# Index queries of rows 64 to 255 alone, and one more sum of four convolution tiles added by a transfer

## The chip, the cores and the metric

The kernel runs on one core of a Trainium2 chip. The metric is the device time of one execution in microseconds (us); a kernel is compared by the median of several executions. All times below are in microseconds unless marked ns.

## The reference

The layer works on 256 rows (tokens) of 1024 numbers in fp32. One projection of the normalized rows gives the inputs of two branches, their gates, and the *index* projections that choose keys:

```python
n = rmsnorm(x, g)
c_a, c_g, q, k, v, qi, ki, wi, gc, ga = split(n @ w_in)
u = c_a * sigmoid(c_g)                       # conv branch: 31 taps, one channel each
y_conv = silu(layernorm(conv31(u) + b)) @ w_conv_out
logits = einsum("bqhd,bsd->bqhs", qi, ki) * 64 ** -0.5     # 8 index heads of 64
score  = einsum("bqh,bqhs->bqs", wi * 8 ** -0.5, relu(logits))
score  = where(key <= query, score, -inf)
idx    = top_k(score, 64)                    # 64 keys for each query row
y_attn = attention(q, k, v over the chosen keys with idx <= query) @ w_attn_out
h = x + (sigmoid(gc + b1) * y_conv + sigmoid(ga + b2) * y_attn) @ w_mix_out
h = h + cross_attention(rmsnorm(h), rmsnorm(mem))          # 256 memory tokens, 4 heads
h = h + relu(rmsnorm(h) @ w1) ** 2 @ w2
out = rmsnorm(h)
```

The query of row r may see keys 0 to r. For rows 0 to 63 that is at most 64 keys, so the top 64 of them are all that they may see, whatever the scores are.

## The kernel before

**Products in two halves.** Every large product is of fp32 numbers written as a sum of two of TensorE's faster 32-bit format (fp32r): `hi`, a rounded copy, and `lo`, what is left. A weight chunk comes from HBM by a transfer on SyncE's queue into one of three buffers `raw`; ScalarE (ACT) copies each 128 columns of it to `hi` (`high`, L315), VectorE (DVE) subtracts to get `lo`. The normalized rows stand the same way in `n_p`, both parts side by side. A tile of 128 output columns takes eight passes over the 1024 inputs with `hi` weights against both parts of the rows (512 columns wide, 256 for each part) and eight *low* passes with `lo` weights against the high part alone (256 columns): `tile_b`, called by `form_b`. The two sums, in one PSUM bank, are put together by a copy on ACT (L481) and an addition on DVE (`merge`). `back` turns the order of passes: in every second tile the low passes come behind the first wide one and not at the end, so that a group of eight low passes of one tile is followed by one wide and the eight low passes of the next. Every instruction that the program gives to TensorE (PE) or DVE passes through a small counting class, so the profile puts all of them on L87; they are told apart by the names of their tiles.

**What runs beside what.** The weights are taken in a fixed order (`STREAM`): four conv tiles, the index queries `qi` (two chunks, four tiles `ps_qi`, L769 to L771), the index keys `ki`, four more conv tiles, the gates, v, then q and k head by head, memory keys and values, and so on to the feed-forward part. Behind each tile, `tick()` advances the side work that is under way by a step: the norm of the memory tokens (`memory`), index scores, attention heads, gates, merges. While a model of DVE's work is behind a model of PE's (`dve.total < pe.total - 1000`, where PE is priced at columns/2.4 ns), `tick` gives DVE the next conv *tap* (`acc<-u,cw,acc`, a multiply-add of a shifted tile) or a round of the choice of keys. Each engine then runs its own list in order, and waits by semaphores.

**The memory norm.** `memory` sums the squares of the memory rows on ACT, turns them to a mean on DVE (`ss_m`), takes the power −0.5 on GpSimd (POOL; `rs_m`, L629), and spreads the result over the partitions by two PE transposes into `ps_mrb`, whose copy (L631) goes on.

**The convolution's sums.** The 31 taps of the eight channel tiles are done in three ways. Most are taps on DVE. Some are products by ACT, two tiles at a time (`products`, L714), which a transfer of GpSimd's queue with an adding end puts onto `acc` (L715). And of tiles 4 to 7 the last 12 taps (`QUADS`) go through `four_tiles` (L673): ACT writes four products of one shift into a slot of `ring` (L683; two slots), and they are added to `four`. The first sums are added by DVE, the last `BY_DMA` = 3 (widths 228, 227 and 226) by transfers on GpSimd's queue (L689). At the end DVE adds `four` to `acc`, then the eight tiles are summed (`usum`) for the layer norm, which starts on PE with `ps_mub`.

**The choice of keys.** `index_scores` takes dot products of `qi_t` with the index keys `ki2`, for the first 128 queries (`qb` = 0) and the next, weights and sums them into `score`; `choose` finds the 64 largest in eight rounds on DVE, and `mask` turns what was found into a tile of large negative numbers `bias` (views of `picked`) that is added to the attention's scores; `causal` fills what lies ahead of the query.

Of the kernel before, what the change touches and what calls it, by code (L numbers as in the profile page):

```python
# [11 lines left out]
AF = mybir.ActivationFunctionType  # L12
ALU = mybir.AluOpType
# [3 lines left out]
P = 128  # L17
D = 1024
S = 256
KT = D // P  # L20
# [3 lines left out]
HD = 128  # L24
XH = 4
K_TOP = 64
IDX_SCALE = float((8 ** -0.5) * (64 ** -0.5))
ATT_SCALE = float(HD ** -0.5)
NEG_FILL = -1.0e38
NEG_TAKEN = -3.4e38  # L30
NEG_BIAS = -1.0e30
# [25 lines left out]
HALVES = 6  # L57
EARLY = (3,)
QUADS = 12
BY_DMA = 3  # L60
PACE = 5
WHOLE = (("conv", 0),)
SEVEN = tuple(range(1, 14))
# [28 lines left out]
class Parts:  # L92
# [5 lines left out]
    def of(self, part, kt, n):  # L98
        t = self.tiles[kt // 4][:, kt % 4 : kt % 4 + n, part, :]
        return t[:, 0, :] if n == 1 else t  # L100

    def high(self, kt, n=1):
        return self.of(0, kt, n)
# [18 lines left out]
def block_kernel(ctx, tc, x, xt, mem, memt, wst, wki, vecs, convw, gout, out):  # L122
    nc = tc.nc
    ctx.enter_context(tc.manual_schedule())
    pe = Counted(nc.tensor, pe_price)
    dve = Counted(nc.vector, dve_price)
    act = nc.scalar.activation
# [5 lines left out]
    lows = ctx.enter_context(tc.tile_pool(name="lows", bufs=HALVES))  # L133
# [4 lines left out]
    def t8(name, dt=F32, shape=(P, KT, S)):  # L138
        return big.tile(list(shape), dt, tag="t8", bufs=12, name=name)

    def parts_t8(name, nkt=KT):
        return Parts([t8(f"{name}{c}", F32R, (P, 4, 2, S)) for c in range(nkt // 4)])

    def w2(name, dt=F32, shape=(P, 512)):
        return work.tile(list(shape), dt, tag="w2", bufs=8, name=name)

    def w4(name, dt=F32, shape=(P, KT, P)):
        return work.tile(list(shape), dt, tag="w4", bufs=2, name=name)
# [4 lines left out]
    def ps_mm(name):  # L153
        return bank("mm", 2, name)
# [4 lines left out]
    def ps_aux(name):  # L159
        return bank("aux", 2, name)  # L160
# [3 lines left out]
    def ps_turn(name):  # L164

        mm_turn[0] += 1
        return (ps_mm if mm_turn[0] % 2 else ps_acc)(name)
# [156 lines left out]
    def split_high():  # L324
        if high_jobs and high_jobs[0].here() and (not high_jobs[0].slot or nsplit[0] - nused[0] < HALVES - held[0]):
            job = high_jobs.pop(0)
            nsplit[0] += job.slot
            while job.steps:
                job.step()
            job.high()  # L330

    def split_low():
        if low_jobs:
            low_jobs.pop(0)()
        for job in high_jobs[:3]:
            if job.steps and job.here():
                job.step()
                break
# [3 lines left out]
    def weights(kind, i, half, kt):  # L342

        key = (kind, i, half)
        while key not in prepared:
            split_high()
            split_low()
        nused[0] += key not in elsewhere
        return [w if kt is None else w.rearrange("p (k n) -> p k n", k=kt) for w in prepared.pop(key)]
# [9 lines left out]
    def add_some():  # L359
        if added and added[0][0] in ready and pe.total >= add_next[0]:  # L360
            pair, pause = added.pop(0)
            add_next[0] = pe.total + pause
            ready[pair]()
            if pair not in [p for p, _ in added]:
                held_back.append((pe.total + 10000, pair))
        if held_back and pe.total >= held_back[0][0]:
            fill.extend(queues.pop(held_back.pop(0)[1]))

    def split_ahead():
        split_low()  # L370
        split_high()

    def tick():
        for c in list(chains):
            if next(c, "end") == "end":
                chains.remove(c)
        while (len(fill) > 1 or (fill and (len(ended) > 5 or nused[0] < 5))) and dve.total < pe.total - 1000:
            fill_one()
        if fours and next(fours[0], "end") == "end":
            fours.clear()  # L380
        dve.total = max(dve.total, pe.total - 2000)
        add_some()

    def fill_one():

        some = [q for q in fill[:3] if q is not turn[0]] or fill
        q = some[0] if len(some[0]) < 10 and len(fill) > 3 else max(some, key=len)
        turn[0] = q
        q.pop(0)()
        if not q:  # L390
            fill.remove(q)
# [5 lines left out]
    def start(gen):  # L397
        chains.append(gen)
        return gen
# [13 lines left out]
    def tile_b(ps, w, x2, kts=range(KT), wide=False, late=False, back=False):  # L413

        ps = ps[: w[0].shape[2]]

        def lows(last):  # L420
            for kt in kts:
                pe.matmul(ps[:, S:], w[1][:, kt, :], x2.high(kt), start=False, stop=last and kt == KT - 1)

        if wide and not late:
            for kt in kts:
                pe.matmul(ps, w[0][:, kt, :], x2.both(kt), start=kt == 0, stop=back and kt == KT - 1)
                if back and kt == 0:
                    lows(False)
            if not back:
                lows(True)  # L430
            return
        for kt in kts:
            wh, wl = w[0][:, kt, :], w[1][:, kt, :]
            if not wide:
                mm_b(ps[:, :S], wh, wl, x2, kt, kt == 0, kt == KT - 1)
            elif kt == 0:
                pe.matmul(ps, wh, x2.both(kt), start=True, stop=False)
                pe.matmul(ps[:, S:], wl, x2.high(kt), start=False, stop=False)
            else:
                pe.matmul(ps[:, S:], wl, x2.high(kt), start=False, stop=False)  # L440
                pe.matmul(ps, wh, x2.both(kt), start=False, stop=kt == KT - 1)

    back = [False]

    def is_wide(kind, ct):

        return kind in ("f1", "qi", "gc", "ga", "ao", "xk", "q", "k") or (kind in ("mix", "co") and ct < 6)

    def form_b(kind, i, x2, after, ps_of=ps_mm):

        for ct in range(2):
            w = weights(kind, i, ct, KT)
            if (kind, i, ct) != ("mix", 3, 1):
                split_ahead()
            ps = ps_of(f"ps_{kind}{i}{ct}")
            wide = is_wide(kind, 2 * i + ct)
            tile_b(ps, w, x2, wide=wide, back=back[0])
            back[0] = wide and not back[0]
            after(2 * i + ct, ps if wide else ps[:, :S])
            tick()  # L460
# [28 lines left out]
    def copy_out(dst, ps, now=False):  # L489
        if ps.shape[1] == S:  # L490
            act(dst, ps, AF.Copy)
        elif now:
            merge_now(dst, ps)
        else:
            start(merge(dst, ps))

    def copy_to(dst):
        return lambda ct, ps: copy_out(dst[:, ct, :], ps)
# [27 lines left out]
    picked = w4("picked", F32, (P, D))  # L526
# [4 lines left out]
    ps = ps_aux("ps_warm")  # L531
# [30 lines left out]
    n2 = parts_t8("n_p")  # L562
# [8 lines left out]
    for rb in range(2):  # L571
        for kt in range(KT):
# [5 lines left out]
                             in1=x_rm[:, 1, D // 2 :], scale=1.0 / D, scalar=EPS, op0=ALU.mult, op1=ALU.add,  # L578
# [21 lines left out]
    for lo, hi in ((0, 1), (1, 2), (2, 4), (4, 6), (6, 8)):  # L600
        dve.tensor_tensor(out=n_f[:, lo:hi, :], in0=xg[:, lo:hi, :],
                          in1=rsb_n.unsqueeze(1).to_broadcast([P, hi - lo, S]), op=ALU.mult)
# [70 lines left out]
    def four_tiles(g):  # L673
# [6 lines left out]
        for n, s in enumerate(taps):  # L680
            dst = ring[:, n % 2, :, s:] if n else sums[:, :, s:]
            for t in range(4):
                act(dst[:, t, :], u[:, 4 * g + t, : S - s], AF.Copy, scale=cw[:, 4 * g + t, TAPS - 1 - s : TAPS - s])  # L683
                if (4 * n + t) % PACE != PACE - 1:
                    yield
            if 0 < n < QUADS - BY_DMA:
                dve.tensor_tensor(out=sums[:, :, s:], in0=sums[:, :, s:], in1=dst, op=ALU.add)
            elif n:
                nc.gpsimd.dma_start(sums[:, :, s:], dst, accum_op=ALU.add)  # L689
        s = taps[0]  # L690
        for _ in range(4 if BY_DMA else 1):
            yield
# [73 lines left out]
            start(memory())  # L766


    qi_t = t8("qi_t", F32, (P, 4, S))  # L769
    for i in range(2):  # L770
        form_b("qi", i, n2, copy_to(qi_t), ps_turn)  # L771
    wk = weights("ki", 0, 0, KT)
    split_ahead()
    ps = ps_mm("ps_ki")
# [3 lines left out]
    wi_t = w2("wi_t", F32, (P, S))  # L778
    act(wi_t[64:NK, :], ps[64:NK, :S], AF.Copy, scale=IDX_SCALE)
    tick()  # L780
    wi = cst.tile([P, 2, 8], F32, name="wi")

    bias = [picked[:, :P], picked[:, P : 3 * P]]
# [6 lines left out]
    def choose(qb, score):  # L790

        def turn(r):
            def go():
                m8 = small.tile([P, 8], F32, tag="m8", name=f"m8_{qb}_{r}")
                dve.max(out=m8, in_=score)
                dve.match_replace(out=score, in_to_replace=m8, in_values=score, imm_value=NEG_TAKEN)
                dve.total += 250
            return go

        def mask():  # L800
            dve.tensor_scalar(bias[qb], score, -3.3e38, NEG_BIAS, ALU.is_gt, ALU.mult)
            causal(bias[qb], qb, NEG_BIAS)

        return [turn(r) for r in range(K_TOP // 8)] + [mask]

# [417 lines left out]
    dst = open_banks("xo")  # L1223
    w = weights("xo", 0, 0, 1)
# [9 lines left out]
    w = weights("xo", 0, 1, 1)  # L1234
# [138 lines left out]
    class Hidden:  # L1373
# [7 lines left out]
        def after(self, ct, ps):  # L1381
            self.jobs.append(start(activation(self.c, ct % 2, ps, self.t, self.hi, self.lo)))
# [249 lines left out]
```

## Time and profile before

| What | us |
|---|---|
| median of 3 runs (497.07 to 497.12) | 497.12 |
| the profiled execution | 497.16 |
| its span, first to last instruction | 495.0 |
| TensorE busy | 487.3 |
| VectorE busy | 460.5 |
| ScalarE busy | 378.4 |
| GpSimd busy | 50.6 |

The mean granted clock of TensorE was 0.998. In rows of a timeline the columns are the start, the duration, the engine (PEld is TensorE's weight load), the line, the operation, what it writes and reads by the program's names, the shapes, and how many neighbours were put together; square brackets hold the engine's idle time just before and what ended it. A row of a tile or a line has the number of instructions and their least, middle and largest duration in ns. The chain gives the share of the span of each engine on the path that ended last.

### The profile page before, as it was taken

The page shows a single profiled execution, that of the slowest core. Times are in us where ns is not written, and L with a number is a line of the kernel's source. Part 1 is how long each engine was busy: PE and PEld are TensorE (multiplying, and loading weights), DVE is VectorE, ACT ScalarE, POOL GpSimd, SP SyncE. Part 2 cuts the span into 40 slices and gives each one's busy share as a digit, 9 for nine tenths or more (in the row PEclk, how much of TensorE's full clock was granted, in tenths as well). Part 3 has the DMA queues.
Part 4 walks back from the last instruction along what each step waited for, and adds up shares of the span by engine and source line. Part 5 has one row for each costly group of instructions (what it writes and reads, how often), then busy time and mean ns, then how long its engine had stood idle before and what let it go on. Part 6 is the DMA issues. An engine that isn't in the chain of part 4 may idle for free.

```text
span 495.0 us, 7793 instructions
## 1 busy us (share of the span) xinstructions
PE 487.3 (98%) x2832; PEld 429.2 (87%) x2832; DVE 460.5 (93%) x828; ACT 378.4 (76%) x678; POOL 50.6 (10%) x67
## 2 busy tenths in 40 slices
PE   8999999999999999999999999999999999999995
PEld 7888888888888889888889999988998888888884
DVE  4999999999999989989988987899999999999986
ACT  5778879999887786767846558687777878888852
POOL 2002212221111211000000000000010101121000
PEclk9999999999999999999999999999999999999999
DMA  8958676989887977354645552866979879999802
GB/s 318 354 215 276 180 190 198 304 245 253 277 219 223 246 176 213 115 171 175 250 169 183 209 204 87 290 189 138 253 274 292 237 242 262 294 333 314 256 9 85
DMA packets 33430, 110.36 MB, mean 223 GB/s; under 512 B 11104, under 2 KB 13408, under 8 KB 24432
## 3 DMA queue, kind: packets, MB, share of 16 engines
q1 hardware_dynamic: 24416, 93.03, 54.4%
q0 software_dynamic: 8688, 16.64, 17.2%
q8 instruction: 22, 0.36, 0.3%
q10 hardware_dynamic: 288, 0.20, 0.1%
q14 instruction: 16, 0.13, 0.1%
HBM read 99.29 MB, written 1.05 MB: 203 GB/s over the span
## 4 chain that ended last, share of the span: by engine, by line
PE 97%; DVE 1%; issue 0%; ACT 0%; DVEq 0%
PE ps_f L87 18%; PE ps_p L87 15%; PE ps_conv L87 9%; PE ps_co L87 5%; PE ps_mix L87 5%; PE ps_ao L87 5%; PE ps_k L87 5%; PE ps_ga L87 5%; PE ps_gc L87 5%; PE ps_q L87 5%; PE ps_v L87 4%; PE ps_xo L87 3%; PE ps_xq L87 2%; PE ps_xk L87 2%; PE ps_qi L87 2%; PE ps_xv L87 2%
## 5 line engine op out<-in xcount | busy, mean ns | idle before, releaser
L87 DVE TENSOR_TENSOR lo<-raw,hi 128x1024 fp32r<-128x1024 f32 x133 | 161.3, 1215 | 2.5 <-ACT hi L315 2.2
L315 ACT ACTIVATE hi<-raw 128x1024 fp32r<-128x1024 f32 x133 | 138.5, 1048 | 6.2 <-DMA raw<-in_wst_dram 6.1
L87 PE MATMUL ps_f<-ff_p,hi 128*128 128x512 f32 (+1 forms) x320 | 72.4, 347 | 0.0
L87 PEld LDWEIGHTS ps_f<-ff_p,hi 128*128 128x128 f32 x320 | 56.2, 189 | 8.2 <-ACT ft L1344 0.3
L87 DVE SCALAR_TENSOR_TENSOR acc<-u,cw,acc 128x241 f32<-128x241 f32 (+23 forms) x142 | 58.5, 465 | 0.1
L87 PE MATMUL ps_f<-ff_p,lo 128*128 128x256 f32 x256 | 46.8, 282 | 0.0
L87 PEld LDWEIGHTS ps_f<-ff_p,lo 128*128 128x128 f32 x256 | 39.3, 191 | 1.8
L715 POOL DMA_DIRECT2D acc<-products x25 | 21.7, 880 | 124.2 <-ACT products L714 59.5
L87 PE MATMUL ps_conv<-n_p,hi 128*128 128x512 f32 x112 | 29.2, 397 | 0.0
L87 PEld LDWEIGHTS ps_conv<-n_p,hi 128*128 128x128 f32 x112 | 20.4, 188 | 4.4 <-issue 0.3
L714 ACT ACTIVATE products<-u,cw 128x243 f32<-128x243 f32 (+19 forms) x50 | 22.1, 492 | 0.0
L293 ACT ACTIVATE inner<-sums 128x1024 fp32r<-128x1024 f32 x13 | 13.8, 1060 | 10.5 <-DVE sums L87 10.5
L87 DVE TENSOR_TENSOR ft<-ft 128x128 f32<-128x128 f32 (+2 forms) x49 | 19.4, 397 | 1.1 <-ACT ft L1344 0.6
L683 ACT ACTIVATE ring<-u,cw 128x236 f32<-128x236 f32 (+10 forms) x44 | 20.2, 480 | 0.0
L87 PE MATMUL ps_p<-outer,fs 128*128 128x512 f32 x78 | 20.1, 393 | 0.0
L87 PE MATMUL ps_v<-hi,n_p 128*128 128x512 f32 x64 | 19.9, 389 | 0.0
L87 PE MATMUL ps_p<-inner,fs 128*128 128x512 f32 x78 | 19.8, 389 | 0.0
L87 PE MATMUL ps_co<-u_p,hi 128*128 128x512 f32 (+1 forms) x80 | 19.3, 350 | 0.0
L87 PE MATMUL ps_mix<-mix_p,hi 128*128 128x512 f32 (+1 forms) x80 | 19.2, 349 | 0.0
L87 PE MATMUL ps_k<-n_p,hi 128*128 128x512 f32 x64 | 17.4, 403 | 0.0
L87 PE MATMUL ps_q<-n_p,hi 128*128 128x512 f32 x64 | 17.3, 402 | 0.0
L87 PEld LDWEIGHTS ps_p<-inner,fs 128*128 128x128 f32 x78 | 14.6, 188 | 3.0
(445 smaller groups left out, 1215.0 us busy)
## 6 DMA issues: line engine op xcount, KB each, us to landing
raw<-in_wst_dram SPq DMA_DIRECT2D x67, 1024.0 KB, 5.7
raw<-in_wst_dram SPq DMA_DIRECT2D x28, 512.0 KB, 6.7
sums<-in_wst_dram POOLq DMA_DIRECT2D x15, 512.0 KB, 8.0
acc<-products POOLq DMA_DIRECT2D x25, 256.0 KB, 5.5
x_rm<-in_x_dram SPq DMA_DIRECT2D x2, 512.0 KB, 4.0
mem_rm<-in_mem_dram SPq DMA_DIRECT2D x1, 1024.0 KB, 7.6
mem_t<-in_memt_dram SPq DMA_DIRECT2D x1, 1024.0 KB, 9.6
h_t<-in_xt_dram SPq DMA_DIRECT2D x1, 1024.0 KB, 7.0
```

The lines of the kernel that those rows point to most:

```text
L87: return fn(*args, **kwargs)
L293: act(hi, src, AF.Copy)
L315: act(hi, raw[:, ns], AF.Copy)
L683: act(dst[:, t, :], u[:, 4 * g + t, : S - s], AF.Copy, scale=cw[:, 4 * g + t, TAPS - 1 - s : TAPS - s])
L714: act(prod[:, a, s:], u[:, t, : S - s], AF.Copy, scale=cw[:, t, TAPS - 1 - s : TAPS - s])
L715: nc.gpsimd.dma_start(acc[:, ts, :], prod, accum_op=ALU.add)
```

## The change

The index queries of rows 0 to 63 are no longer computed (`FREE` = 64). A new `tile_behind` has the same order of passes as `tile_b` and the same turns of `back`, but takes the rows from 64 on: the wide passes read two pieces of 192 columns (384), the low ones 192. The merge has 192 columns. The first 64 rows of `qi_t` are set to zero once, and of the bias tile of the first 128 queries the rows 0 to 63 (`picked[:FREE, :P]`), by two memsets on GpSimd that wait for nothing; `mask` then writes rows 64 to 127 alone for `qb` = 0, and `causal` fills what lies ahead as before.

`BY_DMA` goes from 3 to 4: the sum of width 229 also leaves DVE and is added by a transfer from the ring's slot. The slots are the same two, so a slot that a transfer reads is written again when that transfer has landed.

Nothing else is written otherwise, but the model of `tick` counts the narrower passes as less PE work, so DVE's taps and ACT's `products` stand at other places in their lists behind the index queries.

```diff
+FREE = K_TOP
-BY_DMA = 3
+BY_DMA = 4
...
+    def behind(self, kt, row):
+        return self.tiles[kt // 4][:, kt % 4, :, row:]
...
+    def tile_behind(ps, w, x2, row, back=False):
+        both = ps.rearrange("p (a n) -> p a n", a=2)
+        def lows(last):
+            for kt in range(KT):
+                pe.matmul(both[:, 1, row:], w[1][:, kt, :], x2.high(kt)[:, row:], start=False, stop=last and kt == KT - 1)
+        for kt in range(KT):
+            lo = row
+            pe.matmul(both[:, :, lo:], w[0][:, kt, :], x2.behind(kt, lo), start=kt == 0, stop=back and kt == KT - 1)
+            if back and kt == 0:
+                lows(False)
+        if not back:
+            lows(True)
...
     qi_t = t8("qi_t", F32, (P, 4, S))
-    for i in range(2):
-        form_b("qi", i, n2, copy_to(qi_t), ps_turn)
+    nc.gpsimd.memset(qi_t[:, :, :FREE], 0.0)
+    nc.gpsimd.memset(picked[:FREE, :P], 0.0)
+
+    def query_part(dst, ps):
+        both = ps.rearrange("p (a n) -> p a n", a=2)[:, :, FREE:]
+        act(dst, both[:, 1, :], AF.Copy)
+        yield
+        dve.tensor_tensor(out=dst, in0=both[:, 0, :], in1=dst, op=ALU.add)
+
+    for ct in range(4):
+        w = weights("qi", ct // 2, ct % 2, KT)
+        split_ahead()
+        ps = ps_turn(f"ps_qi{ct}")
+        tile_behind(ps, w, n2, FREE, ct % 2 == 1)
+        start(query_part(qi_t[:, ct, FREE:], ps))
+        tick()
...
         def mask():
-            dve.tensor_scalar(bias[qb], score, -3.3e38, NEG_BIAS, ALU.is_gt, ALU.mult)
+            rows = slice(0 if qb else FREE, P)
+            dve.tensor_scalar(bias[qb][rows], score[rows], -3.3e38, NEG_BIAS, ALU.is_gt, ALU.mult)
             causal(bias[qb], qb, NEG_BIAS)
```

More of the change, by code (lines that the diff above doesn't have):

```diff
@@ L769, in block_kernel @@
     qi_t = t8("qi_t", F32, (P, 4, S))
-    for i in range(2):
-        form_b("qi", i, n2, copy_to(qi_t), ps_turn)
+    nc.gpsimd.memset(qi_t[:, :, :FREE], 0.0)
[12 more added lines that the diff above has]
+        tick()
+    assert not back[0]
     wk = weights("ki", 0, 0, KT)
```

## The prediction

> **What bounds the kernel now.** I read the page first (busy time, then the chain of waits), then the timeline of TensorE around the index queries, then the engines that feed it there, and last the stage in which the moved sum falls. All times are microseconds. The page says where the end comes from:
>
> ```profile
> PE 487.3 (98%) x2832; PEld 429.2 (87%) x2832; DVE 460.5 (93%) x828; ACT 378.4 (76%) x678; POOL 50.6 (10%) x67
> ...
> PE 97%; DVE 1%; issue 0%; ACT 0%; DVEq 0%
> ```
>
> TensorE (PE) is busy for 98% of the span and holds 97% of the chain that ended last. A microsecond taken from PE's stream comes off the end, unless PE then waits for something; a microsecond taken from VectorE (DVE) is worth nothing while PE is still fed. The profiled execution took 497.16, its span 495.0, so 2.16 lie outside the span; the median of the runs shown is 497.12, or 0.04 lower. The sum below is made against 497.16.
>
> The stage that the change narrows is that of the index queries, four tiles `ps_qi`. In PE's timeline the columns are start, duration, what ran, and how many:
>
> ```profile
> 31.80 1.98 PE L87 MATMUL ps_qi<-n_p,hi 128*128 128x512 f32 x8
> 33.61 1.12 PE L87 MATMUL ps_qi<-n_p,lo 128*128 128x256 f32 x8
> 34.56 0.40 PE L87 MATMUL ps_qi<-n_p,hi 128*128 128x512 f32 x1
> ...
> 39.18 1.11 PE L87 MATMUL ps_qi<-n_p,lo 128*128 128x256 f32 x8
> 40.24 0.43 PE L87 MATMUL ps_mrb<-ident,rs_m 128*128 128x128 f32 x2
> ```
>
> Passes overlap, so what a pass costs is its distance from the next start and not its duration: eight wide passes (33.61 − 31.80)/8 = 0.226 apart, eight low ones (34.56 − 33.61)/8 = 0.119 apart. The last eight low passes should therefore be through at 39.18 + 8 × 0.119 = 40.13, but `ps_mrb`, the next piece of work, starts at 40.24. That 0.11 is the only place in this stage where PE doesn't follow itself, and the forecast hangs on it. `ps_mrb` takes `rs_m` from GpSimd (POOL):
>
> ```profile
> 38.20 0.91 POOL L715 DMA_DIRECT2D acc<-products  x1 [30.33 <-ACT products L714]
> 38.84 1.35 POOL L629 TENSOR_TENSOR rs_m<-ss_m,half 128x2 f32<-128x2 f32 x1
> ...
> 228.94 0.71 POOL L538 TENSOR_TENSOR rs_vr<-ms_vr,half 128x2 f32<-128x2 f32 x1 [37.21 <-DVE ms_vr L87]
> ```
>
> `rs_m` ends at 38.84 + 1.35 = 40.19, and PE's next start is 0.05 later: PE already waits for GpSimd there. The same operation with nothing ahead of it (`rs_vr`) takes 0.71, so here it stood 0.6 behind the issue of the `acc` transfer.
>
> **The change, part by part. The wide passes.** 256 more columns cost 0.226 − 0.119 = 0.107, or 0.418 ns a column. 384 columns instead of 512 save 128 × 0.418 = 0.0535 a pass, × 8 = 0.43 a tile, 1.71 for four. That a pass now reads two pieces of 192 I price at nothing: a wide pass already reads two parts side by side.
>
> **The low passes.** 64 columns at the same rate would be 0.027 a pass. But each pass loads its own 128x128 weights, and other rows show what a pass costs that is narrower than its load: three passes of 128 columns and four loads beside passes of 2 columns (PEld is the weight load):
>
> ```profile
> 173.12 0.49 PE L87 MATMUL ps_pt<-ident,att_p 128*128 128x128 f32 x3
> ...
> L87 PE MATMUL ps_pt<-ident,att_p x24: 270/272/273, 168.7 to 215.4; 128*128 128x128 f32 x24
> ```
> ```profile
> 227.57 0.54 PEld L87 LDWEIGHTS ps_vr<-onesd,vs 128*128 128x128 f32 x4
> ...
> 40.24 0.19 PEld L87 LDWEIGHTS ps_mrb<-ident,rs_m 128*128 128x128 f32 x2
> ```
>
> One pass of 128 columns takes 0.27, three take 0.49, so they stand (0.49 − 0.27)/2 = 0.11 apart; with 2 columns the four loads stand at most (0.54 − 0.19)/3 = 0.117 apart. A narrower pass doesn't get under about 0.11. So a low pass saves 0.119 − 0.11 = 0.009, × 8 = 0.07 a tile and 0.29 for four; the ends are nothing and 0.86 (32 × 0.027), and I take 0.29, since 128 columns is the nearer row. The Trainium skill ("TensorE: Matmul & The Clock Gate", section "Back-to-back issue gap") gives an isolated gap of N/2.4 + 2.5 ns and says that in a stream weight load and pass set the spacing together. By the isolated gap alone (an estimate: 82.5 ns for 192 columns) a tile would gain 0.29 on these passes, and the forecast would come out 0.22 lower; the rows at 0.11 speak for the load.
>
> Together PE's own work shrinks by 1.71 + 0.29 = 2.0.
>
> **What of it is kept.** The order of PE's work around `ps_mrb` doesn't move. Before and now, from the last low passes of the third tile (`ps_qi` with a running number) to the fourth tile:
>
> ```order
> L87 MATMUL ps_qi_481<-n_p_125,lo_0_355 128x256 x4
> L87 MATMUL ps_mrb<-ident,rs_m 128x128 x2
> L87 MATMUL ps_qi_518<-n_p_124,hi_1_381 128x512
> L87 MATMUL ps_qi_518<-n_p_124,lo_1_382 128x256 x4
> L87 MATMUL ps_qi_518<-n_p_125,lo_1_382 128x256 x4
> ```
> ```order
> L88 MATMUL ps_qi_480<-n_p_125,lo_0_355 128x192 x4
> L88 MATMUL ps_mrb<-ident,rs_m 128x128 x2
> L88 MATMUL ps_qi_512<-n_p_124,hi_1_381 128x2x192
> L88 MATMUL ps_qi_512<-n_p_124,lo_1_382 128x192 x4
> L88 MATMUL ps_qi_512<-n_p_125,lo_1_382 128x192 x4
> ```
>
> Three tiles still stand ahead of `ps_mrb`, one behind it. PE will be there three tiles' gain, 3 × 0.50 = 1.50, sooner, so what decides is whether `rs_m` also comes sooner. It stands behind the `acc` issue on POOL's queue, which waits for `products` from ScalarE (ACT); its own input is `ss_m` from DVE:
>
> ```profile
> 36.48 0.36 ACT L481 ACTIVATE qi_t<-ps_qi 128x256 f32<-128x256 f32 x1
> 36.74 0.86 ACT L714 ACTIVATE products<-u,cw 128x236 f32<-128x236 f32 x2
> 37.51 1.05 ACT L315 ACTIVATE hi<-raw 128x1024 fp32r<-128x1024 f32 x1
> ```
> ```profile
> 36.15 1.63 DVE L87 SCALAR_TENSOR_TENSOR acc<-u,cw,acc 128x246 f32<-128x246 f32 x4
> ...
> 38.37 0.16 DVE L87 TENSOR_SCALAR ss_m<-ss_m 128x2 f32<-128x2 f32 x1
> ```
>
> ACT runs these one behind the other without a wait, so what releases `products` is ACT's own queue and not PE. The only thing that gets shorter in it is the copy of 192 instead of 256 columns: (1.05 − 0.36)/768 = 0.9 ns a column, × 64 = 0.06. `ss_m` was ready at 38.53, 0.31 before `rs_m` started. So `rs_m` ends at about 40.13 instead of 40.19, and of the 1.50 only 0.06 gets past `ps_mrb`. The fourth tile stands behind it and keeps its 0.50. **Sum: −0.06 − 0.50 = −0.56, 497.16 → 496.60.**
>
> DVE's order does move there. The planner counts PE's work cheaper and puts two conv taps behind `ss_m` that stood ahead of it; before and now:
>
> ```order
> L87 SCALAR_TENSOR_TENSOR acc<-u,cw,acc 128x250
> L87 SCALAR_TENSOR_TENSOR acc<-u,cw,acc 128x245
> L87 SCALAR_TENSOR_TENSOR acc<-u,cw,acc 128x249
> L87 TENSOR_TENSOR lo_0_415<-raw_236,hi_0_414 128x576
> L87 TENSOR_SCALAR ss_m<-ss_m 128x2
> ```
> ```order
> L88 SCALAR_TENSOR_TENSOR acc<-u,cw,acc 128x250
> L88 TENSOR_TENSOR lo_0_417<-raw_236,hi_0_416 128x576
> L88 TENSOR_SCALAR ss_m<-ss_m 128x2
> L88 TENSOR_TENSOR qi_t<-ps_qi_419,qi_t 128x192
> L88 SCALAR_TENSOR_TENSOR acc<-u,cw,acc 128x245
> ```
>
> `ss_m` comes two taps sooner, (1.63/4) × 2 = 0.8. That helps only if `ss_m` and not the `acc` issue holds `rs_m`; it is the first rival.
>
> **What is hidden.** The narrower merges (`qi_t`, 0.4 each on DVE) and the sum that leaves DVE free DVE time, which PE doesn't wait for:
>
> ```profile
> L87 DVE TENSOR_TENSOR four<-four,ring x8: 1104/1123/1129, 99.4 to 157.6; 128x944 f32<-128x944 f32 x1, 128x940 f32<-128x940 f32 x1, 128x936 f32<-128x936 f32 x1, 128x932 f32<-128x932 f32 x1
> ...
> DMA to landing us min/median/max: 5.4/6.2/10.5
> ```
>
> So 1.1 leaves DVE. The two memsets stand on POOL ahead of the first `products`, where it was idle for 30.33 before its `acc` issue. The planner's later taps fall due before the layer norm, whose `ps_mub` must not wait for `usum`:
>
> ```profile
> 216.29 0.87 DVE L87 TENSOR_TENSOR usum<-usum,acc 128x256 f32<-128x256 f32 x2
> ```
> ```profile
> 218.89 0.60 PE L87 MATMUL ps_mub<-usum,onesd 128*128 128x256 f32 x2
> ```
>
> `usum` ends 218.89 − 217.16 = 1.73 ahead. Three taps (0.41 each) and one more `usum` (0.43) now stand in DVE's order between the last attention output and `ps_mub`, where two `usum` stood: 1.66 instead of 0.87, and the 1.1 taken off DVE lies before them: covered. If that cover were gone, PE would lose tenths.
>
> **The rivals. R1, faster: `ps_mrb` waits less.** If `rs_m` is held by its input, it ends 0.8 sooner, and the sum is −0.56 − 0.8 = −1.36: 495.8. If it isn't held at all, the whole 2.0 comes through: 495.2. For it: the operation alone takes 0.71, not 1.35, and POOL's spans may hold waiting. Against: `ss_m` was 0.31 ahead, while `rs_vr` started 0.09 after its input,
>
> ```profile
> 228.70 0.15 DVE L87 TENSOR_SCALAR ms_vr<-ps_vr 128x2 f32<-128x2 f32 x1
> ```
>
> and the queue ahead of it has not moved. Chance 0.23.
>
> **R2, slower: the added transfer holds ACT.** POOL's queue late in the convolution, with what each issue waits for, before and now (a sum of four tiles is `four`, its columns at the end):
>
> ```order
> L715 DMA acc<-products 128x512 [waits DMASW6_49,Activation_49]
> L715 DMA acc<-products 128x512 [waits DMASW7_49,DMASW0_49,Activation_49]
> L715 DMA acc<-products 128x512 [waits DMASW0_49,Activation_49]
> L689 DMA four_923<-ring_924 128x4x228 [waits DVE_49,PE_49,Activation_49]
> L689 DMA four_923<-ring_924 128x4x227 [waits DMASW2_49,Activation_49]
> ```
> ```order
> L735 DMA acc<-products 128x512 [waits DMASW6_49,Activation_49]
> L709 DMA four_912<-ring_913 128x4x229 [waits DVE_49,DMASW0_49,PE_49,Activation_49]
> L735 DMA acc<-products 128x512 [waits DMASW7_49,Activation_49]
> L735 DMA acc<-products 128x512 [waits DMASW1_49,Activation_49]
> L709 DMA four_912<-ring_913 128x4x228 [waits DMASW0_49,Activation_49]
> L709 DMA four_912<-ring_913 128x4x227 [waits DMASW3_49,Activation_49]
> ```
>
> The 229 is new, between `acc` issues that stood together, and the 228 now has a landing (DMASW0) to wait for that it had not. With landings one behind another, what follows is late by one transfer. The profile of before has:
>
> ```profile
> 157.02 0.86 POOL L715 DMA_DIRECT2D acc<-products  x1 [5.62 <-ACT q L481]
> 161.66 0.86 POOL L715 DMA_DIRECT2D acc<-products  x1 [3.78 <-ACT products L714]
> 166.90 0.86 POOL L715 DMA_DIRECT2D acc<-products  x1 [4.38 <-DMA acc<-products]
> 167.44 1.66 POOL L689 DMA_DIRECT2D four<-ring  x1
> ```
> ```profile
> 180.45 0.86 ACT L683 ACTIVATE ring<-u,cw 128x226 f32<-128x226 f32 x2
> ...
> 183.69 0.49 ACT L955 ACTIVATE ptr<-ps_pt 128x384 f32<-128x384 f32 x1 [1.43 <-PE ps_pt L87]
> ```
> ```profile
> 186.95 0.83 PE L87 MATMUL ps_o<-ptr,v_rm 128*128 128x128 f32 x6
> ```
>
> The 228 issued at 167.44 landed at latest 10.5 on, at 177.9. One transfer more ahead of it, about 5 by the distance of the `acc` issues (4.64 and 5.24), makes 183, 182.4 with the 0.56; ACT's ring write of width 226 needs that slot at 180.45 − 0.56 = 179.9. So ACT will wait up to 2.5 in its queue, and behind it stand the next halves of weights and `ptr`, for which PE waits. The cover is ACT's idle 1.43 before `ptr` and the 186.95 − 184.18 = 2.77 from its end to `ps_o`, 4.2 in all. It decides from 4.2 of ACT's waiting, that is a landing past 184.1, and makes the kernel slower by more than 0.2% from 184.1 + 0.56 + 0.99 = 185.7. With the median 6.2 of `four` instead of 5 nothing shows; with its longest, 10.5, the landing is 187.9, PE waits 3.8, and the time is 496.60 + 3.8 = 500.4. Chance 0.09. The Trainium skill ("DMA: Bandwidth & Descriptors", section "Anatomy of one DMA — SWDGE (gpsimd) path") has 2.0 plus bytes/436e3, an estimate of 3.1 for these 0.47 MB; by that ACT would not wait at all, but the rows of this kernel start at 5.4.
>
> **R3, slower: narrow passes of this number format cost double.** No wide-format pass under 256 columns is in the trace. The plain fp32 product is:
>
> ```profile
> L87 PE MATMUL ps_conv<-xg,raw 128*128 128x256 f32 x32 | 7.3, 381 | 0.0
> ```
>
> 7.3/32 = 0.228 a record, two records a product, 1.78 ns a column. Should pieces of 192 fall to that rate, a low pass costs 0.34 instead of 0.119, 32 × 0.22 = 7.1 more, less 1.71: 502.5. Nothing in the trace asks for it. Chance 0.05.
>
> **How the numbers follow.** The forecast, 496.6 by 497.16 − 0.56 and 497.12 − 0.56, has 0.63. 0.2% (0.99, about what a measurement of this kernel can tell from no change) puts the bounds at 496.1 and 498.1, so the forecast counts as the same; R1 is faster, R2 and R3 slower. Chances: faster 0.23, same 0.63, slower 0.14. The range runs from R1's end with the whole gain, 495.2, to 497.6, where the early end of R2 costs a whole 1.0; the rest of the slower cases is left out.
>
> **What would show it right or wrong.** Right: in PE's timeline wide passes 0.172 and low ones 0.11 apart; PE idle for about 1.5 before `ps_mrb`, released by POOL's `rs_m` at about 40.13; the fourth tile 0.50 shorter; no idle PE near 184 to 187 and none before `ps_mub`. Wrong: `rs_m` ending before 39.5 (R1), ACT waiting more than 4.2 at a ring write with PE idle behind it (R2), low passes farther than 0.119 apart (R3), or PE idle at another place.

## The result, and the profile after

| | median | runs | lowest to highest |
|---|---|---|---|
| before | 497.12 | 12 | 496.94 to 497.73 |
| changed | 501.01 | 12 | 497.06 to 503.55 |

The measured ratio of changed to before is 1.006 (95% interval 1.0031 to 1.0089), and the medians lie 3.89 apart, 0.8%. The change is slower by either, and its median is outside the range that was given. It also spreads over 6.5 us, where the kernel before stays within 0.8. Ratios here and below leave out runs more than 1.5% above the fastest of their kernel and medians count all; on the chips of the experiments the kernel before, too, has a few runs at 501 to 504.4 with a clock of 0.992 to 0.995 (5 of 30, 4 of 36, 2 of 13), which widen the intervals there.

The 12 runs fall apart by their mean granted clock: two at 0.999 (497.06 and 497.43), six at 0.993 to 0.995 (498.84 to 501.97), four at 0.991 or 0.992 (502.25 to 503.55). The profiled one took 502.60, its span 500.5, clock 0.991. It shows two places where time and clock are lost. First the chain of its page and TensorE's waits (us in all, times, longest):

```profile
PE 86%; DVE 5%; DMA 3%; ACT 2%; issue 1%; POOL 1%; DVEq 0%; POOLq 0%; ACTq 0%
```
```profile
PE ps_o L88 <- ACT ptr L992: 2.1, 1, 2.1
PE ps_mrb L88 <- POOL rs_m L649: 2.1, 1, 2.1
```

Of the chain only 86% is TensorE's now, and there are two waits that before did not have. Here is TensorE at the index queries:

```profile
31.74 1.57 PE L88 MATMUL ps_qi<-n_p,hi 128*128 128x384 f32 x8
33.15 1.03 PE L88 MATMUL ps_qi<-n_p,lo 128*128 128x192 f32 x8
34.02 0.36 PE L88 MATMUL ps_qi<-n_p,hi 128*128 128x384 f32 x1
...
37.71 1.03 PE L88 MATMUL ps_qi<-n_p,lo 128*128 128x192 f32 x8
40.88 0.43 PE L88 MATMUL ps_mrb<-ident,rs_m 128*128 128x128 f32 x2 [2.13 <-POOL rs_m L649]
41.06 0.52 PE L88 MATMUL ps_qi<-n_p,hi 128*128 128x384 f32 x1
41.38 1.86 PE L88 MATMUL ps_qi<-n_p,lo 128*128 128x192 f32 x8
43.03 2.16 PE L88 MATMUL ps_qi<-n_p,hi 128*128 128x384 f32 x7
45.03 0.40 PE L88 MATMUL ps_ki<-n_p,hi 128*72 128x256 f32 x2
```

Wide passes stand (33.15 − 31.74)/8 = 0.176 apart, low ones (34.02 − 33.15)/8 = 0.109: a tile is 0.48 shorter. Then TensorE waits 2.13 for `rs_m`. But the eight low passes of the fourth tile take 1.86 where those of the third took 1.03, with no wait between them. The windows say why (columns: the window, its length, the busy times of PE, PEld, DVE, ACT and POOL with their numbers of instructions, then TensorE's granted clock as a share of the full one, the DMA share and GB/s):

```profile
31.70:38.58 6.88, 6.88 (x49) 6.83 (x48) 6.85 (x15) 6.85 (x15) 0.49 (x1) 1.00 0.60 194
38.58:40.88 2.30, 0.17 (x3) 0.01 (x1) 2.30 (x6) 1.01 (x2) 2.24 (x2) 1.00 1.00 367
40.88:42.00 1.12, 1.12 (x7) 1.12 (x7) 1.12 (x3) 0.66 (x2) 0.00 (x0) 0.67 0.79 219
42.00:43.00 1.00, 1.00 (x6) 1.00 (x6) 1.00 (x4) 1.00 (x3) 0.00 (x0) 0.50 0.83 260
43.00:44.00 1.00, 1.00 (x5) 1.00 (x4) 1.00 (x3) 0.69 (x2) 0.00 (x0) 0.50 0.88 299
44.00:45.00 1.00, 1.00 (x5) 1.00 (x5) 0.99 (x2) 0.00 (x0) 0.00 (x0) 0.67 1.04 285
45.00:46.00 1.00, 1.00 (x11) 0.97 (x9) 0.41 (x2) 0.77 (x3) 0.00 (x0) 1.00 1.10 322
```

Behind the gap TensorE runs at half clock, for 1.12 × 0.66 + 2.0 + 0.66 = 3.4 us in all, which costs half of that, 1.7 by this count. GpSimd shows why `rs_m` was even later than forecast:

```profile
38.09 0.91 POOL L735 DMA_DIRECT2D acc<-products  x1 [29.79 <-ACT products L734]
38.73 2.09 POOL L649 TENSOR_TENSOR rs_m<-ss_m,half 128x2 f32<-128x2 f32 x1
```

It starts 0.11 sooner than before but lasts 2.09 and not 1.35, and ends at 40.82. The second place is in the attention heads. ACT's ring write, and TensorE behind it:

```profile
167.75 0.47 ACT L703 ACTIVATE ring<-u,cw 128x228 f32<-128x228 f32 x1
174.61 0.48 ACT L703 ACTIVATE ring<-u,cw 128x227 f32<-128x227 f32 x1 [6.38 <-DMA four<-ring]
175.00 1.04 ACT L319 ACTIVATE hi<-raw 128x1024 fp32r<-128x1024 f32 x1
175.94 0.47 ACT L992 ACTIVATE ptr<-ps_pt 128x384 f32<-128x384 f32 x1
```
```profile
176.46 0.94 PE L88 MATMUL ps_o<-ptr,v_rm 128*128 128x128 f32 x6 [2.14 <-ACT ptr L992]
...
177.80 1.91 PE L88 MATMUL ps_k<-n_p,lo 128*128 128x256 f32 x8
...
181.90 0.83 PE L88 MATMUL ps_o<-ptr,v_rm 128*128 128x128 f32 x6
```

The write of width 227 waits 6.38 for the landing of the new transfer of 229, TensorE 2.14 for `ptr`, and then the passes are again at nearly half speed (eight low ones in 1.91, before in 1.11; the windows there give 3.4 us at half clock once more). The chain of waits has what came ahead of that landing:

```profile
157.25 6.61 DMA acc<-products
...
164.98 9.60 DMA four<-ring
```

The same places before, for the account:

```profile
43.31 0.40 PE L87 MATMUL ps_ki<-n_p,hi 128*72 128x256 f32 x2
...
172.45 0.83 PE L87 MATMUL ps_o<-ptr,v_rm 128*128 128x128 f32 x6
...
176.24 0.83 PE L87 MATMUL ps_o<-ptr,v_rm 128*128 128x128 f32 x6
```

The changed kernel is behind by 40.88 − 40.24 = 0.64 at `ps_mrb`, by 1.72 at `ps_ki`, by 4.01 at the first of these `ps_o`, by 5.66 at the second, and by 500.5 − 495.0 = 5.5 at the end. So the first place leaves the kernel 1.72 behind although the four tiles gained 1.9 there, and the second costs 2.3 by waiting and 1.65 by the clock.

### The profile page after: what moved, and what is told of

Same layout as the page of the kernel before. It is cut to its first block, busy times and chain, and to the rows that moved or that the text cites. A ratio compares the mean times of both kernels' runs of the same rounds, so it can differ in the third digit from the quotient of the medians.

```text
span 500.5 us, 7797 instructions
## 1 busy us (share of the span) xinstructions
PE 488.4 (98%) x2832; PEld 431.3 (86%) x2832; DVE 459.9 (92%) x827; ACT 378.8 (76%) x678; POOL 54.1 (11%) x70
## 4 chain that ended last, share of the span: by engine, by line
PE 86%; DVE 5%; DMA 3%; ACT 2%; issue 1%; POOL 1%; DVEq 0%; POOLq 0%; ACTq 0%
PE ps_f L88 18%; PE ps_p L88 15%; PE ps_conv L88 5%; PE ps_co L88 5%; PE ps_mix L88 4%; PE ps_ao L88 4%; PE ps_ga L88 4%; PE ps_gc L88 4%; PE ps_v L88 4%; PE ps_k L88 3%; PE ps_xo L88 3%; PE ps_q L88 3%; PE ps_xq L88 2%; PE ps_xk L88 2%; PE ps_xv L88 2%; DMA four<-ring 2%
## 5 line engine op out<-in xcount | busy, mean ns | idle before, releaser
L88 DVE SCALAR_TENSOR_TENSOR acc<-u,cw,acc 128x241 f32<-128x241 f32 (+26 forms) x142 | 58.5, 464 | 0.1
L88 PEld LDWEIGHTS ps_f<-ff_p,lo 128*128 128x128 f32 x256 | 39.3, 191 | 1.8
```

The lines of the kernel that those rows point to most:

```text
L88: return fn(*args, **kwargs)
```

## The experiments

The theory: two waits, each of which costs its own length and, in part of the runs, 3.4 us at half clock behind it. Rivals: one place alone does it; the second wait is a result of the first; the half clock has another cause.

**The narrower queries alone.**

```diff
-BY_DMA = 4
+BY_DMA = 3
```

> The changed kernel with the sum of width 229 back on VectorE. Theory: ps_mrb still waits about 2.1 for rs_m, and nothing waits near the ring. Without a fall of the granted clock behind that wait the time is 497.12 + 0.64 - 0.48 = about 497.3, with one (3.4 us at half clock, 1.7 lost) about 499.0. Rival, that the ring transfer alone makes the change slow and ps_mrb costs only its own length as forecast: 496.6 and a clock of 0.998 in every run.

Measured: 500.68 (498.88 to 507.23, 7 runs), 1.006 of before (1.0041 to 1.0079). TensorE's wait at the ring's place is gone and `ps_mrb` waits 2.2. With the half clock behind it, `ps_mrb` to `ps_ki` takes 4.15; with three slots and at full clock (below) it takes 2.56, so 1.59 is lost. But a third place appeared that no theory had: `ps_co` waits for `u_p`, the layer norm's result, and the profiled execution falls 1.75 further behind there. So the rival of the ring alone falls, and the number was missed by that third wait: two runs without the half clock, 498.88 and 499.00, are where 497.3 + 1.75 puts them. One at 500.26 with a clock of 0.999 is not explained.

**The sum by transfer alone**, in the kernel before.

```diff
-BY_DMA = 3
+BY_DMA = 4
```

> The kernel before with the sum of width 229 added by a transfer, nothing else. Theory: ScalarE's ring write of width 227 waits for the landing of the 229, TensorE waits for ptr by tenths to 2 us, and in some runs the granted clock falls behind that wait: 497.1 to 501, spread out, clock 0.998 or 0.995. Rival, that the added transfer is hidden and only the moved order of the narrower kernel brings it out: 497.1 in every run.

Measured: 499.47 (497.93 to 503.85, 12 runs), 1.0052 (1.0022 to 1.0082). Slower by itself, without a narrower pass anywhere. In the profiled execution (about the fastest) ACT waits 1.78 at the write of 227, and the cover holds, that is, `ptr` still comes in time and TensorE does not wait at `ps_o`. In four of the 12 the time is over 501. The rival that the transfer is hidden falls by the time; at which place the slower runs lose it is not shown, since none of them was profiled.

**The spread two steps later** (behind the index keys), all else as changed.

```diff
         nc.gpsimd.tensor_tensor(out=rs_m, in0=ss, in1=half, op=ALU.pow)
         yield
+        yield
+        yield
```

> The changed kernel with the spread of rs_m (ps_mrb) two steps later, behind the index keys. Theory: the wait for rs_m is gone and the 2.0 of narrower passes come through up to the ring, where the wait of 2 and at times the clock (1.7) stay or grow: 495.1 + 2.1 to 495.1 + 3.8, so 497.2 to 499, one fall of the clock at most. Rival, that the two waits are one (a late start makes the second): 495.1.

Measured: 499.46 (495.62 to 505.39, 12 runs), 1.0012 (0.9976 to 1.0048). No wait at `ps_mrb`; TensorE is 2.2 ahead of before at `ps_ki`, waits 2.3 at the same `ps_o`, and runs at half clock behind it. The second wait is not a result of the first. The median is above the 497.2 to 499 that were expected: three runs, 503.27 to 505.39, have a clock of 0.991 or 0.992, too low for one stretch of 3.4 us at half clock, which takes 1.7/500 = 0.0034 off the mean. The fastest run, 495.62, would fit a transfer that lands in time; it was not profiled.

**Both undone.**

```diff
-BY_DMA = 4
+BY_DMA = 3
...
+        yield
+        yield
```

> Both undone: the sum of width 229 on VectorE and the spread two steps later. Theory: the whole of the narrower passes, 4 x 0.48 = 1.9, so 495.2, clock 0.998 in every run. Rival, that a wait comes in at another place when TensorE is 2 us ahead (usum, weights): 496 or more with TensorE idle there.

Measured: 497.41 (496.57 to 505.65, 12 runs), 0.9995 (0.9972 to 1.0018). No gain, and the third place is why. TensorE's passes of this kernel, and those of before:

```profile
219.78 0.59 PE L88 MATMUL ps_mub<-usum,onesd 128*128 128x256 f32 x2
...
240.42 0.39 PE L88 MATMUL ps_co<-u_p,hi 128*128 128x512 f32 x1
...
244.29 0.72 PE L88 MATMUL ps_co<-u_p,hi 128*128 128x512 f32 x2 [0.34 <-DVE u_p L88]
...
247.52 2.23 PE L88 MATMUL ps_co<-u_p,hi 128*128 128x512 f32 x9
```
```profile
242.31 0.39 PE L87 MATMUL ps_co<-u_p,hi 128*128 128x512 f32 x1
...
247.71 2.26 PE L87 MATMUL ps_co<-u_p,hi 128*128 128x512 f32 x9
```

TensorE reaches `ps_co` 1.89 sooner than before and leaves it 0.19 sooner. `ps_mub` stands at 219.78, against 218.89 before, although TensorE is 1.9 ahead at the last `ps_o`: VectorE ends `usum` at 218.87 (217.16 before), the layer norm begins a tile later in TensorE's order, and it becomes the bound. With the sum of width 229 on the transfer it doesn't (no `ps_co` wait in the profile of any of those kernels). So the two halves of the change belong together in these orders: narrower queries without a lighter VectorE give their gain back at the layer norm.

**A third slot in the ring** (and fewer small buffers, to make room).

```diff
-        return work.tile(list(shape), dt, tag="w2", bufs=8, name=name)
+        return work.tile(list(shape), dt, tag="w2", bufs=6, name=name)
...
-        return work.tile(list(shape), dt, tag="w4", bufs=2, name=name)
+        return work.tile(list(shape), dt, tag="w4", bufs=3, name=name)
...
+        more = w4(f"more{g}", F32, (P, 4, S))
+        slots = [ring[:, 0], ring[:, 1], more]
...
-            dst = ring[:, n % 2, :, s:] if n else sums[:, :, s:]
+            dst = slots[n % 3][:, :, s:] if n else sums[:, :, s:]
```

> The changed kernel with a third slot in the ring (and 6 instead of 8 small work buffers, to make room). Theory: ScalarE no longer waits for the landing of the 229, no wait near ps_o, VectorE has its 1.1 less, so the layer norm is not late; what is left is ps_mrb: 497.3 without a fall of the clock, 499.0 with one. Rival, that the landings themselves hold another reader (the final sum of four): TensorE waits before ps_mub and the time is over 499 with a clock of 0.998.

Measured: 498.16 (497.26 to 499.25, 12 runs), 0.9996 (0.997 to 1.0022). Exactly two groups: six runs at a clock of 0.998 or more, 497.26 to 497.71, and six at 0.993 to 0.996, 498.60 to 499.25. Their medians, 497.33 and 498.90, are 1.57 apart, for the 1.7 worked out from 3.4 us at half clock. The profiled execution is of the first group:

```profile
41.15 0.43 PE L88 MATMUL ps_mrb<-ident,rs_m 128*128 128x128 f32 x2 [2.17 <-POOL rs_m L649]
...
43.71 0.40 PE L88 MATMUL ps_ki<-n_p,hi 128*72 128x256 f32 x2
```

The gap is the same, and the clock is 1.00 in the microseconds behind it. The second group was not profiled; its times and mean clocks are those of one stretch at half clock. So the same gap brings the half clock in about one run of two.

**Filling the wait**, in the kernel with three slots, with 18 needless transposes (the edit shown), and with 9.

```diff
-    def spread(cols, name):
+    def spread(cols, name, filler=0):
         ps = ps_aux(f"ps_{name}")
+        for _ in range(filler):
+            nc.tensor.transpose(ps[:, S : S + P], ident, ident)
...
-        act(mrb, spread(rs_m, "mrb"), AF.Copy)
+        act(mrb, spread(rs_m, "mrb", 18), AF.Copy)
```

> Three slots, the spread where the change has it, and 18 needless transposes of 128 columns ahead of it (18 x 0.11 = 2.0), so that TensorE works while it would wait. Theory that the wait costs twice, by itself and by the granted clock behind it: rs_m ends when it did, the fourth tile then runs at full clock: 497.3 in every run, clock 0.997 or more, against 497.3 to 499.0 without the filling. Rival, that the half clock has another cause than the gap: it falls here too, 499.0 at 0.994.

> As the filled one with 9 transposes (1.0): a gap of about 1.1 is left. If any gap of a microsecond brings the half clock it falls as often as with 2.1 (499.0, clock 0.994); if only longer ones do, 497.3 in every run.

Measured: 497.29 (497.06 to 497.90, 12 runs) with 18 and 497.32 (497.11 to 498.10, 12 runs) with 9, no run under a clock of 0.996. TensorE's row of the second:

```profile
38.73 1.14 PE L578 MATMUL ps_mrb<-ident 128*128 128x128 f32 x9
41.05 0.43 PE L88 MATMUL ps_mrb<-ident,rs_m 128*128 128x128 f32 x2 [1.18 <-POOL rs_m L651]
```

`rs_m` is no sooner and the tiles no shorter, yet the slow half of the runs is gone. A gap of 1.18 brought the half clock in none of 12 runs, one of 2.2 in six of 12. So in these kernels the half clock comes from the gap and depends on its length. It is not the only way to a low clock: the kernel before, without such a gap, had four of 36 runs at 501 to 504 and 0.992 to 0.995 on the same chip, and what slowed those is open.

**Three slots and the spread two steps later** (the edits of both).

> Three slots, and the spread of rs_m two steps later. Theory: no wait is left, and the 1.9 to 2.0 of narrower passes arrive at the end: 495.2, clock 0.997 to 0.999 in every run. Rival, that a third wait comes in when TensorE is 2 us ahead, as in the kernel with the sum on VectorE, where ps_co waited for u_p: 497.

Measured: 495.57 (494.84 to 504.32, 12 runs), 0.9948 (0.9926 to 0.997). The gain of the narrower passes arrives, 1.7 of the 1.9 by the medians (497.26 before on that chip), with the clock at 0.996 or more in eleven of the runs (the twelfth took 504.32). The rival of a third wait falls for this pair: `ps_co` does not wait.

**The power ahead of the first products**: the same three slots, the spread where the change has it, and the first `acc` issue a step later.

```diff
-    add_next, ready, held_back = [0.0], {}, []
+    add_next, ready, held_back = [32000.0], {}, []
```

> Three slots, the spread where the change has it, and the first products with their acc issue one step later, so that GpSimd has nothing ahead of rs_m. If the queue holds rs_m, it starts 0.1 behind ss_m (37.6) and ends at 38.4 to 38.7, and ps_mrb waits at most 0.1: 495.2. If VectorE's work beside it is what stretches it (0.71 alone, 1.35 and 2.09 so far), it starts at 37.6 but ends when the instructions on VectorE allow it, 39 to 40, and ps_mrb still waits 0.5 to 1.5: 495.7 to 496.7.

Measured: 495.40 (494.86 to 495.91, 5 runs), 0.9961 (0.9948 to 0.9974). GpSimd's row and TensorE's:

```profile
37.95 0.69 POOL L649 TENSOR_TENSOR rs_m<-ss_m,half 128x2 f32<-128x2 f32 x1 [29.89 <-DVE ss_m L88]
```
```profile
38.74 0.40 PE L88 MATMUL ps_mrb<-ident,rs_m 128*128 128x128 f32 x2
```

With nothing ahead of it `rs_m` takes 0.69, VectorE being as busy as elsewhere, and ends at 37.95 + 0.69 = 38.64; `ps_mrb` follows the third tile without a wait. So the queue holds it.

**VectorE idle beside the power**, with three slots, behind the `acc` issue (the edit shown), and with the power first. A copy on VectorE reads `rs_m`, so VectorE waits until the power is done.

```diff
+    seen = cst.tile([P, 2], F32, name="seen")
...
         nc.gpsimd.tensor_tensor(out=rs_m, in0=ss, in1=half, op=ALU.pow)
+        nc.vector.tensor_copy(out=seen, in_=rs_m)
```

> Three slots, the spread and the acc issue where the change has them, and behind ss_m a copy on VectorE that reads rs_m, so that VectorE does nothing while GpSimd works on it. If VectorE's work stretches rs_m, it now takes about 0.7 and ends at about 39.5 to 39.8, and ps_mrb waits 1.0 instead of 2.2. If rs_m is long because of the acc issue ahead of it, it still takes 1.3 to 2.1 and ends at 40.2 to 40.8. VectorE loses about 2 and TensorE may wait for it later, so the time is not the question.

> Both: nothing ahead of rs_m on GpSimd and VectorE idle while it runs. rs_m should take 0.71 and end at about 38.4, ahead of TensorE's arrival at 38.6, with no wait at ps_mrb: 495.2, if the 0.8 that VectorE gives away is covered later.

Measured: behind the issue (one run, 497.51) GpSimd has

```profile
38.12 0.91 POOL L739 DMA_DIRECT2D acc<-products  x1 [29.83 <-ACT products L738]
38.77 1.02 POOL L650 TENSOR_TENSOR rs_m<-ss_m,half 128x2 f32<-128x2 f32 x1
```

1.02, the rest of the issue (0.26) and the operation's own 0.7 or so, in place of 2.09: what is above that in the changed kernel is there only with VectorE at work, by this one profile. With nothing ahead, 495.70 (495.29 to 496.15, 6 runs), 0.9967 (0.9954 to 0.9979): no better than without the copy, since 0.69 is all that the operation takes there anyway. VectorE's work alone does not stretch it either, as the kernel before this one shows (0.69). Which instruction of VectorE does it stays open; of the kernels with the issue ahead, the 2.1 stands in every one where a weight subtraction begins on VectorE at 39.0 to 39.3 beside it, and the 1.33 to 1.35 where four taps ran.

**Two slots of the three**, all else as with the power first.

```diff
-            dst = slots[n % 3][:, :, s:] if n else sums[:, :, s:]
+            dst = slots[n % 2][:, :, s:] if n else sums[:, :, s:]
```

> The kernel with nothing ahead of rs_m and three slots (495.4), with one thing put back: only two of the three slots are used, all sizes and buffers as there. Theory: ScalarE waits again for the landing of the 229 at its ring write of width 227, TensorE for ptr behind it by 0 to 3, in some runs with a fall of the clock: 495.4 to 500, spread out. Rival, that the smaller number of work buffers and not the slot made the difference: 495.4 with no spread.

Measured: 500.37 (494.75 to 503.73, 10 runs), 1.0027 (0.9985 to 1.007). ACT waits 5.2 at the write of 227 in the profiled execution, TensorE 1.4 at `ps_o`; six of ten runs are at 500 or more with a clock of 0.991 to 0.994, the others at 494.75 to 497.09. The median is just above the 495.4 to 500 that were expected. With all three slots and the same buffers the runs were at 494.86 to 495.91 (the power first, on another chip), so the slot made the difference, not the number of work buffers.

## Why the prediction was wrong

**The passes: right.** Wide passes 0.176 apart for 0.172, low ones 0.109 for 0.11; a tile 0.48 shorter for 0.50. The row of 128 columns was the right one to take for the low passes.

**What holds `rs_m`: right in part.** TensorE waits at `ps_mrb`, since the `acc` issue stands ahead of `rs_m` on GpSimd's queue; the kernel with the power first shows it. R1, with `ss_m` as what holds it, falls: `ss_m` was two taps sooner and `rs_m` began only 0.11 sooner.

**"`rs_m` ends at about 40.13": mis-sized.** It ended at 40.82. I took its 1.35 along unchanged, and put all that is above 0.71 down to the `acc` issue, though the order of VectorE beside it changes; the taps that moved away make room for a subtraction, and the operation lasts 2.09 (1.02 behind the issue with VectorE idle). That is 0.69 later than 40.13, and it makes the forecast without any half clock 496.6 + 0.7 = 497.3, which is what three slots give at full clock (497.33).

**A wait priced at its own length alone: the first step that failed.** A wait of 1.5 was forecast and set off against the gain as if TensorE went on behind it as before. In this profile it doesn't: 3.4 us at half clock follow at each of the two places, and 1.6 to 1.7 is lost each time. The sum put this term at nothing without a reason. At `ps_mrb`, filling the gap removes it. The profile ends 5.5 behind before, where the sum had 0.56 ahead; of these 6.1 the longer `rs_m` is about 0.7, the clock 3.2 and the wait at `ps_o` 2.3. The range had no room for any of the three.

**The landing taken as covered: the second step that failed.** The sum has no wait at `ps_o`, and R2, which has one, was right in mechanism but wrong in place and chance. ACT's ring write does wait for the landing, behind it `ptr`, then TensorE at `ps_o`, and the cover was near: 6.38 of waiting less 2.14 that came through is 4.24, and 4.2 was worked out for the write after it. But I looked at the 228 and the write of 226, and gave one transfer more as 5 later. What decided is the 229 itself and the write of 227 before it: the issue at 164.98 stood behind an `acc` issue that waited for a landing of 6.61, and itself took 9.60. A third slot removes this wait and two of the three bring it back; the sum by transfer alone is slower, too (1.0052). The case had 0.09 and belonged among the likely cases. Its time, 500.4, is near the measured 501.01 by luck: it had 3.8 of waiting and no fall of the clock.

**`usum` covered: right for the change, its loss mis-sized.** The 1.66 is not in place of the 0.87, as I wrote, but on top of it, so the cover of 1.73 was nearly used up; `usum` ends at 224.23 in the changed kernel, 0.32 ahead of `ps_mub`. I priced the loss of the cover at tenths. With the sum back on VectorE it is 1.7 at `ps_co`: 1.89 ahead, 0.19 left.

**R3: did not come about.** Low passes of 192 columns stand 0.109 apart and not 0.34.

## What to carry to other kernels

When a bound engine's work shrinks, look first for what it will now arrive at too soon, and price that wait twice: by its length and by what the clock does behind it. The idle time that a row shows is a cover only while the order around it stays; an operation's duration, too, can depend on its neighbours on other engines. A transfer that reads a ring's slot makes the next writer of the slot wait for a landing, so the slot count has to go with the transfers. With that and with the power ahead of the first products, the narrower queries do pay: 495.40, 0.9961 of before (0.9948 to 0.9974).

## What the runs showed of the hardware

- In the profiles, gaps of 2.13, 2.14, 2.16 and 2.29 us in TensorE's work were followed by about 3.4 us at half granted clock, and gaps of 2.17, 1.42, 1.18 and 1.09 were not. By the mean clock, six of 12 runs of the kernel with the gap of 2.17 had such a fall, and none of 12 with 1.18. The Trainium skill ("TensorE: Matmul & The Clock Gate", section "What's actually happening") has the clock fall after at least one idle window of about 3.4 us. Here the stretch at half clock is about as long as that window, 3.4, but the gap that brings it is shorter than the window.
- A 128x2 power on GpSimd took 0.69 with nothing ahead, 1.02 behind a transfer's issue with VectorE idle, and 1.33 to 2.10 behind it with VectorE at work.
